# w_out 512 columns wide, eight early pairs, and another first and last chunk in the down stage of a hybrid layer

## The chip, the cores and the metric

The kernel runs on one core of one Trainium2 chip. The metric is the device time of one execution in microseconds (us), as the median of several executions. One further execution is profiled; the rows in this document come from its trace, with times counted from the start of its span. The engines are TensorE (PE, matmuls; PEld is its weight load), VectorE (DVE), ScalarE (ACT), GpSimd (POOL) and SyncE (SP), which here issues nearly all DMAs in the order of its queue.

## What is computed

One post-norm decoder layer on 1024 tokens of width 1024: three token mixers in parallel (a gated linear recurrence, sliding window attention and attention into a memory), their gated sum through `W_out`, a LayerNorm, a squared-ReLU MLP of inner width 4096, and a second LayerNorm. All inputs and outputs are float32. Cut to what the change touches:

```python
merged = (gates[:, :, 0] * (o_a @ w_branch_hg[layer])
          + gates[:, :, 1] * (o_b @ w_branch_swa[layer])
          + gates[:, :, 2] * (o_c @ w_branch_mem[layer]))
mix = merged @ w_out[layer]
h = layer_norm(alpha * h + mix, ln1_g[layer], ln1_b[layer])
ff = jnp.square(jax.nn.relu(h @ w_up[layer])) @ w_down[layer]
h = layer_norm(alpha * h + ff, ln2_g[layer], ln2_b[layer])
```

## The kernel before

**Products.** Every float32 operand is split into a high part, which ScalarE casts (L74), and a low part, the rest, which GpSimd or VectorE subtracts (L75). A product is then three matmuls: high by high, high by low, low by high (`mm`, L59). Two operands of 128x1024 or so therefore cost one cast and one subtraction each before TensorE can use them. SBUF is divided into pools whose names appear in the rows: R holds raw loads (four buffers in rotation), W split weights, X, O, MG, BT and T large operands, G and S small ones; PSUM has three z, three s and two t banks. A tile in a pool's next buffer waits until the tile that held the buffer was last read.

**Mixers, in two halves of 512 tokens** (`hf` = 0, 1): window attention, memory attention, recurrence, then w_out (L627 to L640). There the merged rows stand still in TensorE and the weight passes through 256 columns at a time (`zn`): 384 matmuls per half, four column groups, each added to the residual rows and its statistics taken on VectorE (L636, L640). LayerNorm (L686 to L690) leaves rows with tokens on partitions, and they have to be transposed for the MLP. Each block of 128 rows has a deferred `flip_h1`: for the second half it loads the first half's transposed block from DRAM (L655, "left", an R buffer), transposes its own on TensorE (L661, "right", another R buffer), and forms the sums and differences that the up stage needs on VectorE and GpSimd (L670 to L676 and L75).

**Up stage.** The two token halves and the two halves of a 256 column pair of `W_up` make a 2 by 2 block product, done with seven products of a Strassen type instead of eight: 12 matmuls of 512 columns each, 84 for each of the 16 pairs (L749 to L809). The first two products of a pair use only the plain halves of the tokens. So three pairs (`EARLY`) do their first two products (`first_two`, L726 to L734) ahead of the flips, and keep the first in a PSUM z bank; then all four flips are emitted, then the loop over the pairs. The seven combinations of each pair's result, needed below, go to DRAM as `d_ff[i, j]`.

**Down stage.** Eight chunks of 512 inner columns, again seven products each (`down`, L851; `operands`, L831), 24 matmuls of 512 columns per product, added into eight accumulators `pa[0..7]` of 128x2048. The chunk's w_down rows come raw into two T buffers (`wd_raw`, L822); between products VectorE combines them in place (128x1024, `add`, L710). Per product one left operand is loaded from `d_ff` into R (L833) and split with its low part on GpSimd, and one combination of w_down is split from T. The counter `turn` goes up by two per product, so it is even wherever it is asked, up to the last two products: all left operands before them go to BT buffers, and all weights' low parts to GpSimd. The last chunk orders its products so that the accumulators of the second half's rows are complete first; `finish_rows` normalises them, and the last two products are run row block by row block, each block followed by its LayerNorm (statistics L906 and L943, then L944 to L962, with GpSimd doing a power at L945 and the last addition at L960).

A scheduler orders each engine's queue from dependences; the code above is the order of emission, not of execution.

## Time and profile before

| | us |
|---|---|
| median of 3 runs | 2197.18 |
| fastest, slowest | 2196.35, 2200.23 |
| profiled execution | 2198.1 |
| its span in the trace | 2196.3 |
| TensorE busy in the span | 2089.0 (95%) |
| VectorE, GpSimd, ScalarE busy | 1113.3, 915.3, 844.1 |

The profiled execution has 1.8 us outside its span. Busy shares are means over stages with different limits: TensorE's 95% is nearly 100% in most stretches and much lower in a few, GpSimd's 42% is 94% in the down stage. A stage's own stretch has to be read to see what limits it. The stages of interest begin at about 1430 us (w_out of the second half), 1476 (early pairs), 1493 (flips), 1535 (loop over pairs), 1821 (down stage) and 2106 (last chunk).

### The profile page before, as it was taken

The page shows a single profiled execution, that of the slowest core. Times are in us where ns is not written, and L with a number is a line of the kernel's source. Part 1 is how long each engine was busy: PE and PEld are TensorE (multiplying, and loading weights), DVE is VectorE, ACT ScalarE, POOL GpSimd, SP SyncE. Part 2 cuts the span into 40 slices and gives each one's busy share as a digit, 9 for nine tenths or more (in the row PEclk, how much of TensorE's full clock was granted, in tenths as well). Part 3 has the DMA queues.
Part 4 walks back from the last instruction along what each step waited for, and adds up shares of the span by engine and source line. Part 5 has one row for each costly group of instructions (what it writes and reads, how often), then busy time and mean ns, then how long its engine had stood idle before and what let it go on. Part 6 is the DMA issues. An engine that isn't in the chain of part 4 may idle for free.

```text
span 2196.3 us, 27345 instructions
## 1 busy us (share of the span) xinstructions
PE 2089.0 (95%) x10602; PEld 1741.6 (79%) x10602; DVE 1113.3 (51%) x2032; ACT 844.1 (38%) x1484; POOL 915.3 (42%) x431
## 2 busy tenths in 40 slices
PE   8999999999999999999999999995999997999982
PEld 8767888898988976688889898893888885888872
DVE  5466242244543466634125444237555553676679
ACT  5344243233333254424224333324555554433321
POOL 2212223422235431122332223554344336999984
PEclk9999999999999999999999999996999998999996
DMA  8311223222224441122332223424444448444412
GB/s 286 122 58 58 92 88 99 96 79 85 79 95 126 162 145 48 58 89 87 99 100 80 83 81 94 155 76 148 159 154 158 154 145 301 146 155 152 136 58 77
DMA packets 100114, 256.06 MB, mean 117 GB/s; under 512 B 8544, under 2 KB 22032, under 8 KB 99984
## 3 DMA queue, kind: packets, MB, share of 16 engines
q1 hardware_dynamic: 99088, 251.16, 35.4%
q10 hardware_dynamic: 896, 3.16, 0.4%
q8 instruction: 83, 1.36, 0.3%
q14 instruction: 47, 0.39, 0.1%
HBM read 212.33 MB, written 41.96 MB: 116 GB/s over the span
## 4 chain that ended last, share of the span: by engine, by line
PE 79%; POOL 9%; DVE 5%; issue 5%; ACT 1%; DMA 1%; SPq 0%; DVEq 0%; POOLq 0%; ACTq 0%
PE pz L59 56%; PE ps L59 17%; POOL W L75 5%; PE pt L59 4%; POOL BT L75 2%; PE pt L272 1%; POOL sm L945 1%; DVE X L710 0%; DVE S L264 0%; ACT BT L74 0%; DVE bn L906 0%; POOL X L960 0%; DVE sm L954 0%; DMA T<-in_w_down_dram 0%; PE pt L528 0%
## 5 line engine op out<-in xcount | busy, mean ns | idle before, releaser
L75 POOL TENSOR_TENSOR W<-R,W 128x1024 fp32r<-128x1024 f32 x198 | 478.1, 2415 | 1037.6 <-ACT W L74 1029.9
L59 PE MATMUL pz<-X,W 128*128 128x512 f32 x3360 | 814.9, 396 | 0.0
L59 PEld LDWEIGHTS pz<-X,W 128*128 128x128 f32 x3360 | 624.9, 189 | 140.4 <-issue 11.5
L74 ACT CAST W<-R 128x1024 fp32r<-128x1024 f32 (+1 forms) x299 | 306.0, 1025 | 386.6 <-PE pz L59 158.2
L59 PE MATMUL pz<-O,W 128*128 128x512 f32 x1152 | 266.8, 390 | 0.0
L59 PEld LDWEIGHTS pz<-O,W 128*128 128x128 f32 x1152 | 215.9, 188 | 45.6 <-issue 0.8
L59 PE MATMUL ps<-W,BT 128*128 128x256 f32 (+1 forms) x1016 | 224.0, 340 | 20.1 <-ACT W L74 13.6
L59 PEld LDWEIGHTS ps<-W,BT 128*128 128x128 f32 x1016 | 175.8, 191 | 42.2 <-ACT W L74 14.0
L75 DVE TENSOR_TENSOR W<-R,W 128x1024 fp32r<-128x1024 f32 (+1 forms) x103 | 129.6, 1259 | 116.5 <-ACT W L74 110.4
L75 POOL TENSOR_TENSOR W<-T,W 128x1024 fp32r<-128x1024 f32 x55 | 147.7, 2687 | 21.3 <-ACT W L74 21.3
L75 POOL TENSOR_TENSOR BT<-R,BT 128x1024 fp32r<-128x1024 f32 x55 | 141.4, 2571 | 23.0 <-ACT BT L74 23.0
L59 PE MATMUL pz<-W,BT 128*128 128x512 f32 x492 | 125.9, 391 | 3.0 <-POOL BT L75 2.5
L74 ACT CAST BT<-R 128x1024 fp32r<-128x1024 f32 (+1 forms) x59 | 60.4, 1024 | 168.1 <-issue 134.5
L59 PE MATMUL ps<-W,T 128*128 128x256 f32 x640 | 121.3, 283 | 0.0
L59 PEld LDWEIGHTS pz<-W,BT 128*128 128x128 f32 x492 | 92.9, 189 | 23.3 <-POOL BT L75 2.9
L373 DVE SCALAR_TENSOR_TENSOR G<-G,pz 128x512 f32<-128x512 f32 x32 | 22.0, 687 | 169.9 <-PE pz L59 169.9
L59 PEld LDWEIGHTS ps<-W,T 128*128 128x128 f32 x640 | 97.3, 192 | 1.2
L59 PE MATMUL pz<-W,X 128*128 128x256 f32 x768 | 93.7, 283 | 0.0
L59 PE MATMUL pt<-O,W 128*128 128x512 f32 x384 | 92.6, 390 | 0.8 <-DVE T L710 0.8
L59 PEld LDWEIGHTS pz<-W,X 128*128 128x128 f32 x768 | 92.9, 192 | 0.3
L59 PEld LDWEIGHTS pt<-O,W 128*128 128x128 f32 x384 | 71.9, 188 | 16.6 <-DVE T L710 1.8
L59 PE MATMUL pt<-W,BT 128*128 128x512 f32 x324 | 84.2, 395 | 0.0
(228 smaller groups left out, 2629.0 us busy)
## 6 DMA issues: line engine op xcount, KB each, us to landing
R<-d_ff SPq DMA_DIRECT2D x56, 512.0 KB, 3.6
R<-in_w_gate_dram SPq DMA_DIRECT2D x48, 512.0 KB, 3.6
R<-in_w_b_dram SPq DMA_DIRECT2D x48, 512.0 KB, 3.5
R<-in_w_up_dram SPq DMA_DIRECT2D x35, 512.0 KB, 4.1
T<-in_w_down_dram SPq DMA_DIRECT2D x16, 1024.0 KB, 5.2
d_ff<-T SPq DMA_DIRECT2D x61, 256.0 KB, 2.9
d_ff<-S SPq DMA_DIRECT2D x48, 256.0 KB, 2.9
R<-in_w_sq_dram SPq DMA_DIRECT2D x16, 512.0 KB, 3.6
```

Source lines behind the costliest of these rows:

```text
L59: nc.tensor.matmul(o, lhsT=l, rhs=r, start=start, stop=stop, skip_group_check=more)
L74: (hi_copy or nc.scalar.copy)(hi, src)
L75: (lo_eng or nc.gpsimd).tensor_tensor(out=lo, in0=src, in1=f32(hi), op=ALU.subtract)
L272: nc.tensor.transpose(o[:, c:c + P], pr[:, 2 * t + i, :], ident)
L373: nc.vector.scalar_tensor_tensor(out=t, in0=t, scalar=1.0, in1=o, op0=ALU.add, op1=ALU.mult)
L945: nc.gpsimd.tensor_tensor(out=y, in0=e, in1=mhalf[:, :1], op=ALU.pow)
```

## The change

1. w_out is laid out 512 columns wide: two column groups of four weights, 192 matmuls of 512 columns per half instead of 384 of 256. Two loads of the next stage's tokens (`load_x`) move to the ends of the two groups, and the statistics are taken over 512 columns.
2. `EARLY` goes from 3 to 8. The first product of an early pair no longer stays in PSUM: it is written to DRAM (`d_p1`) and read back in the loop, where VectorE adds it (`plus`) in place of ScalarE's copy. Two flips are emitted ahead of pair 3, two ahead of pair 4.
3. The first chunk of w_down goes into an X buffer. The accumulators are grouped otherwise, their residual rows are loaded after the first product's operands, and GpSimd subtracts one accumulator from another once (128x2048).
4. `turn` goes up by one per product: left operands alternate between BT and MG, the weights' low parts between GpSimd and VectorE.
5. The last chunk is done by plain products, one row block after the other: 8 blocks of 24 matmuls, 192 in place of 168, each followed by its LayerNorm. The combinations of the accumulators move into the seventh chunk, the scale and shift vectors are loaded later, and the last two pairs write one more result (`d_ff[i, 0]`) to DRAM.

```diff
+EARLY = 8
...
-        for cg in range(4):
-            oo = [pt("s"), pt("s")]
-            for c in range(2):
-                w = weight(a["w_o"][2 * cg + c])
-                zn(oo, w, c, mhi[c], mlo[c])
...
+        for f in range(2):
+            oo = [pt("ssst"[n] if f == 0 else "zzzt"[n]) for n in range(4)]
+            cols = slice(f * 512, (f + 1) * 512)
+            for c in range(4):
+                w = weight(a["w_o"][4 * f + c])
+                for n in range(4):
+                    ts = slice(n * P, (n + 1) * P)
+                    for e in range(2):
+                        k = 2 * c + e
+                        rh, rl = w[:, 0, e * 512:(e + 1) * 512], w[:, 1, e * 512:(e + 1) * 512]
+                        lh, ll = mhi[k // 4][:, k % 4, ts], mlo[k // 4][:, k % 4, ts]
+                        mm(oo[n], lh, rh, k == 0, False)
+                        mm(oo[n], lh, rl, False, False)
+                        mm(oo[n], ll, rh, False, k == NK - 1)
+            load_x(nsrc, f + 2, nx, nc.vector)
+            for n in range(4):
+                rv = r[n // 2][:, n % 2, cols]
+                nc.vector.scalar_tensor_tensor(out=rv, in0=rv, scalar=2.0 * ALPHA, in1=oo[n], op0=ALU.mult,
+                                               op1=ALU.add)
+                nc.vector.bn_stats(out=bn[n][:, f, :], in_=rv)
...
+        nc.sync.dma_start(d_p1[i], s1)
...
-        deferred.pop(0)()
+
+    for i in range(EARLY):
+        if i in (3, 4):
+            deferred.pop(0)()
+            deferred.pop(0)()
+        first_two(i)
...
+            p1 = st("G", [P, TH])
+            nc.sync.dma_start(p1, d_p1[i])
...
+        o = pt("z")
         if i >= EARLY:
-            o = pt("z")
...
+        prod(o, w4, 0, 6, i < EARLY)
+        s2 = snap(o) if i >= EARLY else plus(o, p1)
         c = pt("s")
         prod(c, w2, 1, 4)
         prod(o, w3, 0, 7, False)
-        s3 = snap(o)
+        s3 = snap(o) if i >= EARLY else plus(o, p1)
...
+            if i >= NFF - 2:
+                nc.sync.dma_start(d_ff[i, 0], f[:, 2, :])
...
     def wd_raw(c):
-        res = []
+        src = a["w_down"][4 * c:4 * c + 4].rearrange("(j m) p d -> m p j d", m=2)
+        if c == 0:
+            t = st("X", [P, 2, 2, 2, TH])
+            res = [t[:, 0], t[:, 1]]
+        else:
+            res = [st("T", [P, 2, 2, TH]) for _ in range(2)]
         for m in range(2):
-            t = st("T", [P, 2, 2, TH])
-            nc.sync.dma_start(t.rearrange("p j f d -> p j (f d)"),
-                              a["w_down"][4 * c:4 * c + 4].rearrange("(j m) p d -> m p j d", m=2)[m])
-            res.append(t)
+            nc.sync.dma_start(res[m].rearrange("p j f d -> p j (f d)"), src[m])
...
-        t = turn[0]
+        if c == 0 and j == 1:
+            acc_pair("X", 1, 2)
+            rows_h1(2, 0, 0)
+            acc_pair("O", 5, 3)
+            rows_h1(5, 1, 1)
+            rows_h1(3, 0, 1)
+            acc_pair("O", 7, 6)
+            nc.gpsimd.tensor_tensor(out=pa[3], in0=pa[3], in1=pa[5], op=ALU.subtract)
+        if c == 0 and j == 4:
+            acc_pair("X", 4, 0)
+            rows_h1(0, 1, 0)
...
-            o = block(f, w, b)
-            if c == 0 and j in (2, 3, 4):
+            o = psum(turn[0] + b)
+            bs = slice(b * P, (b + 1) * P)
+            for jj in range(2):
+                mm(o, f[:, 0, jj, bs], w[:, 0, jj, :], jj == 0, False)
+                mm(o, f[:, 0, jj, bs], w[:, 1, jj, :], False, False)
+                mm(o, f[:, 1, jj, bs], w[:, 0, jj, :], False, jj == 1)
...
-        turn[0] = t + 1
...
-        down(c, 2, b21)
-        down(c, 5, b11)
+        if c < NC - 2:
+            down(c, 2, b21)
+            down(c, 5, b11)
+            add(b12, b22, b12, ALU.subtract)
+            down(c, 3, b22)
+            down(c, 7, b12)
+            add(b22, b22, b11, ALU.subtract)
+            down(c, 6, b22)
+            add(b21, b21, b22, ALU.subtract)
+            down(c, 4, b21)
+            if c == 1:
+                nc.vector.scalar_tensor_tensor(out=pa[4], in0=pa[0], scalar=ALPHA, in1=pa[4], op0=ALU.mult,
+                                               op1=ALU.add)
+            continue
         add(b12, b22, b12, ALU.subtract)
+        down(c, 7, b12)
         down(c, 3, b22)
-        down(c, 7, b12)
         add(b22, b22, b11, ALU.subtract)
         down(c, 6, b22)
+        add(pa[6], pa[6], pa[1])
+        add(pa[7], pa[7], pa[6])
+        down(c, 2, b21)
         add(b21, b21, b22, ALU.subtract)
+        down(c, 5, b11)
+        add(pa[6], pa[6], pa[5])
+        add(pa[5], pa[5], pa[7])
         down(c, 4, b21)
...
+        add(pa[4], pa[4], pa[7])
+
+    lng, lnb = ln_consts(nc, st, a["ln2_g"], a["ln2_b"])
+    ffs, wds = [], []
+    for j in range(2):
+        for m in range(2):
+            i = NFF - 2 + j
+            raw = st("R", [P, 2, TH])
+            nc.sync.dma_start(raw[:, 0], d_ff[i, (1, 2)[m]])
+            nc.sync.dma_start(raw[:, 1], d_ff[i, (0, 4)[m]])
+            f = st("MG" if m else "BT", [P, 2, S], F32R)
+            split(f[:, 0], f[:, 1], raw.rearrange("p h t -> p (h t)"), nc.gpsimd)
+            ffs.append(f)
+            wds.append(weight(a["w_down"][2 * i + m], nc.vector if m else nc.gpsimd))
+    add(pa[3], pa[3], pa[6])
     add(pa[2], pa[2], pa[1])
...
+    for b in (4, 5, 6, 7, 0, 1, 2, 3):
+        bs = slice(b * P, (b + 1) * P)
...
+        parts = []
+        for ch in range(2):
+            cs = slice(ch * TH, (ch + 1) * TH)
+            o = psum(turn[0])
+            turn[0] += 1
+            for e in range(4):
+                mm(o, ffs[e][:, 0, bs], wds[e][:, 0, cs], e == 0, False)
+                mm(o, ffs[e][:, 0, bs], wds[e][:, 1, cs], False, False)
+                mm(o, ffs[e][:, 1, bs], wds[e][:, 0, cs], False, e == 3)
+            v = pa[((2, 3), (4, 5))[b // 4][ch]][:, b % 4, :]
+            add(v, v, o)
+            nc.vector.bn_stats(out=bn[:, ch, :], in_=v)
+            parts.append((v, cs))
+        layer_norm(nc, small, parts, bn[:, 0:2, :], lng, lnb, LN_EPS, mhalf,
+                   lambda cs, v, b=b: nc.sync.dma_start(outv[b][:, cs], v), b != 3)
```

The scheduler's queues show where this puts the work. First SyncE around the flips. Before (L655 loads a flip's left block, L718 a raw w_up weight, L742 and L754 store and reload results), from the second flip's load on:

```order
L655 DMA R_1470_11891<-d_h1t_82 128x8x128
L742 DMA d_ff_81<-G_1465_11857 128x512
L655 DMA R_1474_11920<-d_h1t_82 128x8x128
L754 DMA T_1482_11978<-d_ff_81 128x512
L754 DMA T_1492_12059<-d_ff_81 128x512
L655 DMA R_1478_11949<-d_h1t_82 128x8x128
L718 DMA R_1483_11979<-in_w_up_dram 128x1024
L718 DMA R_1484_11982<-in_w_up_dram 128x1024
L718 DMA R_1493_12060<-in_w_up_dram 128x1024
```

After, the same place (L663 is the flip's load, L731 the weight, L744 and L750 store the early pairs' two results):

```order
L663 DMA R_1470_11495<-d_h1t_83 128x8x128
L750 DMA d_ff_81<-G_1465_11461 128x512
L731 DMA R_1474_11524<-in_w_up_dram 128x1024
L766 DMA T_1512_11777<-d_ff_81 128x512
L663 DMA R_1480_11563<-d_h1t_83 128x8x128
L663 DMA R_1484_11592<-d_h1t_83 128x8x128
L744 DMA d_p1_82<-G_1477_11542 128x512
L731 DMA R_1488_11621<-in_w_up_dram 128x1024
L731 DMA R_1494_11660<-in_w_up_dram 128x1024
L750 DMA d_ff_81<-G_1479_11558 128x512
L766 DMA T_1524_11861<-d_ff_81 128x512
L731 DMA R_1500_11699<-in_w_up_dram 128x1024
```

One weight load (R_1474, pair 3) now stands ahead of the loads of the third and fourth flip, and those of pairs 4 to 6 behind them.

Second, GpSimd where the up stage ends, the low halves of left operands (BT, MG) and weights (W). Before, from the last up weight (W_1714) on:

```order
L75 TENSOR_TENSOR W_1714_13969<-R_1709_13952,W_1714_13969 128x1024
L75 TENSOR_TENSOR BT_1735_14134<-R_1734_14132,BT_1735_14134 128x1024
L75 TENSOR_TENSOR BT_1742_14175<-R_1741_14173,BT_1742_14175 128x1024
L75 TENSOR_TENSOR W_1736_14137<-T_1732_14128,W_1736_14137 128x1024
L75 TENSOR_TENSOR W_1743_14178<-T_1733_14130,W_1743_14178 128x1024
```

After, from the last up weight (W_1740) on:

```order
L76 TENSOR_TENSOR W_1740_13622<-R_1735_13605,W_1740_13622 128x1024
L76 TENSOR_TENSOR MG_1764_13824<-R_1763_13822,MG_1764_13824 128x1024
L76 TENSOR_TENSOR MG_1778_13905<-R_1777_13903,MG_1778_13905 128x1024
L76 TENSOR_TENSOR BT_1754_13776<-R_1753_13774,BT_1754_13776 128x1024
L76 TENSOR_TENSOR BT_1771_13864<-R_1770_13862,BT_1771_13864 128x1024
L76 TENSOR_TENSOR W_1755_13779<-X_1752_13771,W_1755_13779 128x1024
L76 TENSOR_TENSOR W_1772_13867<-X_1752_13771,W_1772_13867 128x1024
L76 TENSOR_TENSOR W_1786_13948<-X_1752_13771,W_1786_13948 128x1024
L868 TENSOR_TENSOR O_1757_13784<-O_1757_13784 128x2048
```

Two MG operands are made first, then two BT operands, and the first three weights are taken from X instead of T; the accumulators' subtraction (L868) follows them.

Third, TensorE in the last chunk. Before, where the last two products go by row blocks (BT and MG are their left operands; a row "x6" is six matmuls):

```order
L59 MATMUL ps_2153_16461<-W_2149_16450,BT_2148_16447 128x512 x6
L59 MATMUL pt_2154_16469<-W_2152_16458,MG_2151_16455 128x512
L59 MATMUL pz_2160_16498<-W_2149_16450,BT_2148_16447 128x512 x6
L59 MATMUL ps_2161_16506<-W_2152_16458,MG_2151_16455 128x512
L59 MATMUL pt_2167_16535<-W_2149_16450,BT_2148_16447 128x512 x6
L59 MATMUL pz_2168_16543<-W_2152_16458,MG_2151_16455 128x512
L59 MATMUL pz_2175_16580<-W_2152_16458,MG_2151_16455 128x512
```

After, from the last product of the seventh chunk (ps_2111) on:

```order
L60 MATMUL ps_2111_15792<-W_2107_15765,BT_2106_15762 128x512 x6
L60 MATMUL ps_2131_15852<-W_2117_15813,BT_2115_15808 128x512 x3
L60 MATMUL ps_2131_15852<-W_2121_15824,MG_2119_15819 128x512 x3
L60 MATMUL ps_2131_15852<-W_2125_15835,BT_2123_15830 128x512 x2
L60 MATMUL pt_2132_15867<-W_2117_15813,BT_2115_15808 128x512 x2
L60 MATMUL ps_2131_15852<-W_2125_15835,BT_2123_15830 128x512
L60 MATMUL ps_2131_15852<-W_2129_15846,MG_2127_15841 128x512
L60 MATMUL pt_2132_15867<-W_2117_15813,BT_2115_15808 128x512
L60 MATMUL pt_2132_15867<-W_2121_15824,MG_2119_15819 128x512 x3
L60 MATMUL pt_2132_15867<-W_2125_15835,BT_2123_15830 128x512 x3
```

Each row block's result now gathers 12 matmuls per 512 columns from four left operands and four weights; the first block starts ahead of the third pair of operands, and TensorE alternates between two results until that pair is there.

## Rows read from the trace of the kernel before

**Rows 1.** The page's busy times: us, share of span, instructions.

```profile
PE 2089.0 (95%) x10602; PEld 1741.6 (79%) x10602; DVE 1113.3 (51%) x2032; ACT 844.1 (38%) x1484; POOL 915.3 (42%) x431
```

**Rows 2.** The chain that ended last: share of the span by engine.

```profile
PE 79%; POOL 9%; DVE 5%; issue 5%; ACT 1%; DMA 1%; SPq 0%; DVEq 0%; POOLq 0%; ACTq 0%
```

**Rows 3.** Table by stretch: us, busy us of each engine (instructions), granted clock, DMA.

```profile
1430.00:1476.20 46.20, 46.20 (x386) 46.16 (x385) 15.51 (x28) 9.01 (x9) 20.76 (x10) 1.00 0.26 81
...
1492.57:1541.03 48.46, 21.15 (x81) 15.61 (x80) 35.15 (x43) 25.34 (x42) 19.81 (x11) 0.65 0.45 146
...
1549.40:1563.23 13.83, 13.83 (x61) 11.19 (x60) 6.38 (x11) 7.32 (x11) 4.82 (x2) 1.00 0.66 210
...
1821.20:1854.69 33.49, 18.18 (x69) 14.02 (x69) 13.66 (x12) 12.95 (x17) 17.54 (x7) 0.75 0.83 306
...
1900.00:2000.00 100.00, 100.00 (x443) 82.84 (x442) 66.65 (x84) 37.55 (x38) 94.28 (x38) 1.00 0.46 150
...
2105.95:2196.30 90.35, 45.64 (x169) 35.19 (x167) 76.93 (x115) 19.23 (x24) 57.65 (x34) 0.75 0.18 64
```

**Rows 4.** Timeline of TensorE, up to down: start, us, [idle before <-releaser].

```profile
1811.88 2.88 PE L59 MATMUL pz<-BT,W 128*128 128x512 f32 x12
...
1818.27 3.04 PE L59 MATMUL pt<-O,W 128*128 128x512 f32 x12 [0.78 <-DVE T L710]
...
1834.92 0.79 PE L59 MATMUL ps<-W,BT 128*128 128x512 f32 x1 [13.62 <-ACT W L74]
```

**Rows 5.** Timeline of TensorE around the flips.

```profile
1492.57 1.03 PE L661 MATMUL pt<-cst,T 128*128 128x128 f32 x8
...
1525.12 1.22 PE L59 MATMUL ps<-T,W 128*128 128x512 f32 x2 [18.09 <-ACT W L74]
```

**Rows 6.** Timeline of SyncE's queue, first weights of the main loop.

```profile
1516.25 22.11 SPq L718 DMA_DIRECT2D R<-in_w_up_dram  x7
```

**Rows 7.** Timeline of VectorE, last reads of two flips' left blocks.

```profile
1503.63 0.68 DVE L75 TENSOR_TENSOR T<-R,T 128x512 fp32r<-128x512 f32 x1
...
1517.43 0.69 DVE L75 TENSOR_TENSOR T<-R,T 128x512 fp32r<-128x512 f32 x1
```

**Rows 8.** The page's groups (busy us, mean ns) and DMA issues (KB, us).

```profile
L75 POOL TENSOR_TENSOR W<-R,W 128x1024 fp32r<-128x1024 f32 x198 | 478.1, 2415 | 1037.6 <-ACT W L74 1029.9
...
L74 ACT CAST W<-R 128x1024 fp32r<-128x1024 f32 (+1 forms) x299 | 306.0, 1025 | 386.6 <-PE pz L59 158.2
...
R<-in_w_up_dram SPq DMA_DIRECT2D x35, 512.0 KB, 4.1
```

**Rows 9.** Timeline of GpSimd and SyncE, up to down.

```profile
1815.71 4.76 POOL L75 TENSOR_TENSOR BT<-R,BT 128x1024 fp32r<-128x1024 f32 x2 [8.27 <-ACT BT L74]
...
1826.54 2.16 SPq L826 DMA_DIRECT2D T<-in_w_down_dram  x2
```

**Rows 10.** Groups from 1900 to 2105: count, busy us, mean ns, idle before.

```profile
L710 DVE TENSOR_TENSOR T<-T,T 128x1024 f32<-128x1024 f32 x13 | 25.5, 1962 | 12.8 <-POOL W L75 12.8
...
L710 DVE TENSOR_TENSOR X<-X,pz 128x512 f32<-128x512 f32 x32 | 21.8, 682 | 10.1 <-PE pz L59 10.1
...
L75 POOL TENSOR_TENSOR W<-T,W 128x1024 fp32r<-128x1024 f32 x38 | 101.8, 2678 | 4.6 <-ACT W L74 4.6
```

**Rows 11.** Groups of VectorE in the last chunk, 2105.95 to the end.

```profile
L710 DVE TENSOR_TENSOR O<-O,O 128x2048 f32<-128x2048 f32 x2 | 6.6, 3310 | 0.0
...
L75 DVE TENSOR_TENSOR W<-T,W 128x1024 fp32r<-128x1024 f32 x1 | 1.2, 1167 | 0.0
```

**Rows 12.** Timeline of TensorE in the last chunk, its longest wait.

```profile
2166.06 2.50 PE L59 MATMUL pt<-W,MG 128*128 128x512 f32 x5 [14.23 <-DVE sm L955]
```

**Rows 13.** Timeline of VectorE, aggregates of the last three row blocks.

```profile
2175.30 0.20 DVE L943 BATCH_NORM_AGGREGATE sm<-bn 128x2 f32<-128x12 f32 x1
...
2181.93 0.20 DVE L943 BATCH_NORM_AGGREGATE sm<-bn 128x2 f32<-128x12 f32 x1
...
2187.67 0.21 DVE L943 BATCH_NORM_AGGREGATE sm<-bn 128x2 f32<-128x12 f32 x1
```

88 lines of the change are left out of this document (15 added, 73 removed).

## Prediction

> **What bounds the kernel now.** I read the page first, then one table by stage, then the timelines around each hole it shows. TensorE is busy 95% of the span [rows 1] and carries 79% of the chain of waits [rows 2], so time can be won in two ways only: fewer or denser matmuls, or shorter holes in its stream. The table by stage [rows 3] shows where the holes are. In a full stretch, 61 matmuls of 512 columns take 13.83 us, 226.7 ns each, and that is the price I use. The stretch 1900 to 2000 has no hole. The stretch around the flips (1492.57 to 1541.03) and the last chunk (2105.95 to the end) have large ones, with the mean granted clock at 0.65 and 0.75. A third hole lies where the up stage passes into the down stage: TensorE stands 13.62 us ahead of its first down product [rows 4]. The diff touches all three, and w_out.
>
> **w_out, 512 wide.** Before, 386 matmuls of 256 columns fill 46.20 us [rows 3], 119.7 ns each. Per half 384 × 0.1197 = 46.0 us becomes 192 × 0.2267 = 43.5 us; two halves give −4.9 us. Same operands, same weight bytes; nothing on that path waits in the stretch, so it counts in full.
>
> The Trainium skill ("TensorE: Matmul & The Clock Gate", section "Back-to-back issue gap") puts the warm gap at N/2.4 + 2.5 ns, 109.2 and 215.8 ns; by it the two halves would win 768 × 0.1092 − 384 × 0.2158 = 1.0 us only. The rows here show a fixed part nearer 13 ns per matmul, so halving their number is worth more; its other figure there, 131 ns for N = 512 in a sustained stream, no stretch of this trace comes near.
>
> **The up gap.** Before, from 1492.57 (call it F, when the third early pair is done and the transposes of the flips begin) to 1541.03 there are 48 matmuls, 10.9 us of work in 48.46 us: 37.6 us lost. TensorE waits for the first weight of the main loop, 18.09 us [rows 5], which SyncE could issue only at 1516.25 [rows 6], because its R buffer belongs to a flip whose DVE work ends late. The change puts five more early pairs, 5 × 24 × 0.2267 = 27.2 us of matmuls, into this hole. But their weights go through the same R buffers behind the same flips: pair 3 takes flip 0's left buffer, last read by the DVE operation at 1503.63 (F+11.8 at its end), pairs 4 and 5 those of flip 2, last read by the one at 1517.43 (F+25.5) [rows 7], and by my estimate 2 us later now, since flip 2's own buffer waits for flip 1's. A weight then needs 4.1 us to land, 1.0 us of cast and 2.4 us on GpSimd [rows 8]. So pair 3 starts near F+19 and pair 4 near F+35.6; four pairs at 21.8 us, the first at half clock (the mean granted clock of this hole is 0.65, so I add 2.7 us), end near F+60, and by then the main loop's weights are ready. Lost: 60.1 − 27.2 = 32.9 us. I take 37.6 − 32.9, so −5 us. Bounds: −27 if the whole 27.2 us drops into the hole, +3 if GpSimd serves the new weights late (one 2.4 us operation).
>
> In the main loop an early pair runs 60 matmuls, 13.60 us, and takes 13.83 [rows 3]: five more cost about 0.2 us each, +1 us. The reload of the first product (256 KB) and two DVE adds of 0.68 us in place of ScalarE copies lie under TensorE: DVE is at 6.4 of 13.83 us there.
>
> **Up to down.** TensorE's last up product ends at 1821.2 (U). The first w_down load goes out only at 1826.54 [rows 9], since its T buffers are held by the last pairs; the first product then starts at 1834.92 and runs in pieces: from U to 1854.69 TensorE does 69 matmuls, 15.64 us of work in 33.49 [rows 3], 17.9 us lost. The change loads this chunk into an X buffer, which is free after the last pair's second product, two groups of 2.72 us ahead of the BT group at 1811.88 [rows 4], so near U−15. Load and cast are then hidden. What remains is GpSimd's queue: two MG operands, two BT operands, whose buffer TensorE reads until 1814.76 [rows 4], and only then the first weight's low half. Two BT operands end at 1820.47 now [rows 9]; 2.4 us for the weight behind them give U+1.7. I count 2 us of stall left, −16 us. Bounds −18 (none left) and −10 (X lands late and three GpSimd operations of 2.6 us stand on the path). The GpSimd add of 128x2048 in this chunk is behind the third weight; I cost it at nothing, because MG operands were made ahead, and at 3 us if that cover is gone.
>
> **Steady down stage.** 49 products stay 24 matmuls, 5.44 us. GpSimd goes from two operations of about 2.6 us per product (95% busy) to one and a half, 3.9 us; DVE gets every second weight's low half. DVE per chunk: 28 × 0.682 = 19.1, four T adds at 1.96 as measured beside a busy GpSimd [rows 10], 3.5 weights between 1.17 [rows 11] and the same 1.96: 31 to 34 us of 38.1. So no change, 0; the upper end is rival three.
>
> **Last chunk.** Before, 90.35 us: 168 matmuls (38.1 us), stalls of which the longest is 14.23 us [rows 12], and rows finished at DVE's pace, 5.74 us from one aggregate to the next, then 8.6 us from the last aggregate to the end [rows 13]. After, let D be TensorE's end of chunk 6. Eight rows of 24 matmuls are 43.5 us, 5.4 more than before. The third BT operand can't start before D and its low half comes about 2.4 us late: TensorE ends at D+45.9. DVE still has four PSUM adds (2.7 us), two 128x2048 adds at 3.3 us [rows 11] and a weight's low half left at D, together some 12.5 us; its first aggregate is near D+14.5, seven periods of 5.7 later D+54.4, end D+63. That is 90.35 − 63 = −27 us. Bounds: D+56 if TensorE sets the pace (45.9 + about 10 for one row), D+67 at 6.3 us a row: −34 to −23.
>
> **Sum.** −4.9 − 5 + 1 − 16 + 0 − 27 = −52 us. The profiled execution took 2198.1 us (span 2196.3 and 1.8 around it), 0.9 above the median of the three runs, 2197.18. So 2145 us beside the median.
>
> **Rivals.**
> One: the early pairs fill the whole up gap, −27 instead of −5: 2123 us. For it: weights wait in W buffers ahead, and the flips might go faster with GpSimd free. Against it: SyncE's order puts the loads of pairs 4 to 7 behind the loads of all four flips, and only four R buffers turn there. Chance 0.12.
>
> Two: the win is smaller at both ends of the down stage. If X lands late the boundary gives −10, not −16; if rows run at 6.6 us (the spacing before the one shown, 2175.30 to 2181.93) the tail ends 6 to 7 us later, and the DVE backlog of chunk 6 (four adds of 3.3 us on top of 34 of 38.1) stalls TensorE by some 6 us: +18, 2163 us. Chance 0.15. For it: one of the two spacings shown is 6.63 us, where GpSimd's adds stood beside DVE's work.
>
> Three, on the other side: DVE becomes the bound of the down stage. Each DVE operation with two SBUF inputs would wait out a whole GpSimd operation of 2.6 us. Per product that is 4 × 0.682 + (7.5/7) × (1.17 + 2.6) = 6.77 us against 5.44; 49 products give +65 us, 2210 us, slower. It decides from a mean wait of 1.36 us per operation (2.73 + 1.07 × (1.17 + w) = 5.44). Against it: T adds took 1.96 us in a stretch where GpSimd was 94% busy, a wait of 0.8 us, and GpSimd will be 70% busy. Chance 0.05.
>
> The Trainium skill ("SBUF — State Buffer", section "SBUF: two separate sides") says that the port pair shared by DVE and GpSimd is an exclusive lock for a whole instruction, also when the DVE operation has two SBUF inputs; that is rival three's mechanism. The trace agrees on the kind (1.17 us alone, 1.96 beside GpSimd), not on the price of a full instruction each time.
>
> **How the numbers follow.** The forecast holds 0.68: its own range, from the bounds that can fall together (up gap −12 to +3, boundary −18 to −10, tail −34 to −23), is about 2130 to 2162. To leave out no more than 2 in 10 the range goes to rival one on the low side and past rival two on the high: 2122 to 2166. 0.2% is 4.4 us, about what runs of this kernel tell from no change (they spread over 3.9 us). Slower than that is rival three, 0.05; within it, a steady down stage some 1 us slower per product, 0.02; faster 0.93.
>
> **What would show it.** w_out: 192 matmuls per half at 227 ns. The flips: two TensorE holes, one ahead of the fourth early pair (15 us or more) and one ahead of the fifth, instead of one of 18. The boundary: a wait of some 2 us on GpSimd ahead of the first down product, and the clock not at 0.50. Steady stage: 5.44 us a product, GpSimd near 70%, DVE near 85%. Tail: DVE rows 5.6 to 5.8 us apart and TensorE ended some 17 us ahead of the end. I am wrong if the up gap vanishes, if products in chunks 1 to 6 are spaced by more than 5.5 us, or if TensorE's last matmul lies within 10 us of the end.

## The result, and the profile after

The changed kernel takes 2172.02 us (median of 4 runs, 2170.84 to 2174.51) against 2196.89 for the kernel before on the same chip: a ratio of 0.9885 with a 95% interval of 0.9868 to 0.9902. It is 25 us faster; 52 were forecast, and the time lies above the forecast's range (2122 to 2166).

Let F be the first transposes of the flips, U the end of the last up product, D the end of the seventh chunk (chunk 6 in the code) on TensorE. The profiled span falls from 2196.3 to 2171.3 us, as follows:

| stretch | before | after | difference | forecast |
|---|---|---|---|---|
| start to F (w_out, both halves) | 1492.57 | 1489.20 | -3.4 | -4.9 |
| F to U (flips, up stage) | 328.6 | 328.8 | +0.2 | -4 |
| U to D (seven chunks) | 284.8 | 281.3 | -3.5 | -16 |
| D to the end (last chunk) | 90.35 | 72.0 | -18.35 | -27 |

The 27 us that are missing lie in the last two rows (12.5 and 8.7 us), in F to U (4.2) and in w_out (1.5).

The page's busy times and the chain that ended last [rows 1, 2] are now these; GpSimd has less on the chain and TensorE more:

```profile
PE 2096.4 (97%) x10242; PEld 1725.8 (79%) x10242; DVE 1141.3 (53%) x2041; ACT 827.8 (38%) x1462; POOL 844.8 (39%) x401
...
PE 84%; DVE 5%; POOL 4%; issue 3%; DMA 2%; ACT 2%; SPq 0%; POOLq 0%; DVEq 0%; ACTq 0%
```

The table by stretch of the kernel after (columns as in [rows 3]) has, in this order, w_out of the second half, the gap from the flips to the loop over the pairs, the first 33 us of that loop, the first 38 us of the down stage, its steady part, and the last chunk:

```profile
1426.65:1472.87 46.22, 46.22 (x205) 38.27 (x204) 17.19 (x21) 10.18 (x11) 21.68 (x11) 1.00 0.30 92
1489.20:1547.57 58.37, 39.19 (x153) 30.25 (x152) 38.51 (x41) 33.57 (x54) 30.37 (x15) 0.77 0.59 192
1547.57:1581.00 33.43, 30.11 (x123) 23.60 (x122) 16.15 (x24) 12.45 (x18) 8.19 (x4) 0.95 0.49 172
1817.98:1855.60 37.62, 31.18 (x121) 24.09 (x120) 26.19 (x26) 15.35 (x21) 21.00 (x8) 0.91 0.79 282
1900.00:2000.00 100.00, 100.00 (x436) 81.68 (x436) 88.77 (x98) 36.01 (x36) 72.21 (x27) 1.00 0.46 146
2099.30:2171.30 72.00, 47.98 (x193) 37.73 (x191) 61.37 (x100) 11.69 (x17) 38.51 (x25) 0.86 0.16 61
```

**The up gap.** TensorE around the flips and at the loop's start (the loop begins at 1547.57 with the MG operand):

```profile
1504.88 1.22 PE L60 MATMUL pz<-X,W 128*128 128x512 f32 x2 [5.83 <-ACT W L75]
...
1520.67 1.22 PE L60 MATMUL pz<-X,W 128*128 128x512 f32 x2 [4.26 <-ACT W L75]
...
1547.57 2.96 PE L60 MATMUL pz<-MG,W 128*128 128x512 f32 x12
...
1555.17 4.17 PE L60 MATMUL pz<-BT,W 128*128 128x512 f32 x12 [1.91 <-DVE G L718]
```

The one wait of 18.09 us [rows 5] has become two pieces ahead of the fourth and the fifth early pair, and the early pairs end at F+58.4, as forecast (F+60). But the loop's first pairs now wait too (1.91 us at 1555.17, 1.41 at 1572.27). VectorE and SyncE show on what:

```profile
1545.93 0.33 SPq L731 DMA_DIRECT2D R<-in_w_up_dram  x1
...
1550.29 1.60 DVE L718 TENSOR_TENSOR R<-R,R 128x512 f32<-128x512 f32 x1 [7.09 <-DMA R<-in_w_up_dram]
...
1554.34 0.68 DVE L718 TENSOR_TENSOR G<-pz,G 128x512 f32<-128x512 f32 x1
```

A raw weight lands late, VectorE stands at its subtraction for 7.09 us, and `plus` (1554.34), which TensorE waits for, stands behind that in VectorE's queue. SyncE sent this weight at 1545.93, just when GpSimd was done with the low half of an early pair's weight (1543.51 to 1545.91) and that weight's R buffer came free.

**Up to down.** TensorE, SyncE and GpSimd at the start of the down stage:

```profile
1817.96 0.39 PE L60 MATMUL ps<-W,BT 128*128 128x512 f32 x1
1820.06 1.42 PE L60 MATMUL ps<-W,BT 128*128 128x512 f32 x5 [1.71 <-POOL W L76]
...
1844.74 2.93 PE L60 MATMUL ps<-W,MG 128*128 128x512 f32 x6 [4.28 <-DVE O L880]
```

```profile
1838.79 0.48 SPq L846 DMA_DIRECT2D T<-in_w_down_dram  x1
...
1838.84 4.53 POOL L868 TENSOR_TENSOR O<-O 128x2048 f32<-128x2048 f32 x1 [8.87 <-DMA O<-d_h]
...
1848.56 0.36 SPq L836 DMA_DIRECT2D X<-d_h  x1
1848.97 0.73 SPq L846 DMA_DIRECT2D T<-in_w_down_dram  x1
```

The wait of 13.62 us [rows 4] is down to 1.71, nearly the 2 forecast. Then GpSimd stands for 8.87 us until residual rows have landed, subtracts, VectorE's next evictions (which empty PSUM banks) stand behind that, and TensorE stands for 4.28 us and then runs twelve matmuls at the lower of its two clock levels (granted clock 0.50 from 1844.74 to 1850.03), 5.3 us instead of 2.8. SyncE stands for 9.3 us at the next residual rows (1848.56), whose X buffer the first chunk uses until GpSimd's last split from it ends at 1848.54, with the raw operands of the second chunk behind it. From U to the 15th product it is 88.1 us against 94.4 before, so of the 11.9 us won at the first product 6.3 are left; the five later chunks then take 38.6 to 38.7 us each instead of 38.08, which costs 2.8.

**The last chunk.** TensorE, GpSimd and VectorE around D = 2099.3:

```profile
2101.84 0.50 PE L60 MATMUL ps<-W,BT 128*128 128x512 f32 x1 [0.68 <-POOL W L76]
...
2110.55 0.80 PE L60 MATMUL ps<-W,BT 128*128 128x512 f32 x1 [7.75 <-POOL BT L76]
```

```profile
2092.66 2.40 POOL L76 TENSOR_TENSOR BT<-R,BT 128x1024 fp32r<-128x1024 f32 x1
2097.39 4.39 POOL L76 TENSOR_TENSOR W<-R,W 128x1024 fp32r<-128x1024 f32 x1 [2.34 <-ACT W L75]
2101.75 4.39 POOL L76 TENSOR_TENSOR MG<-R,MG 128x1024 fp32r<-128x1024 f32 x1
2106.10 4.40 POOL L76 TENSOR_TENSOR BT<-R,BT 128x1024 fp32r<-128x1024 f32 x1
```

```profile
2097.26 2.28 DVE L718 TENSOR_TENSOR X<-X 128x2048 f32<-128x2048 f32 x1
2099.47 4.47 DVE L718 TENSOR_TENSOR O<-O,O 128x2048 f32<-128x2048 f32 x1
2103.86 0.67 DVE L718 TENSOR_TENSOR X<-X,ps 128x512 f32<-128x512 f32 x1
2104.46 3.83 DVE L718 TENSOR_TENSOR O<-O,O 128x2048 f32<-128x2048 f32 x1
...
2111.51 2.28 DVE L718 TENSOR_TENSOR X<-X,O 128x2048 f32<-128x2048 f32 x1
2113.71 2.28 DVE L718 TENSOR_TENSOR O<-O,O 128x2048 f32<-128x2048 f32 x1
2117.96 0.69 DVE L718 TENSOR_TENSOR X<-X,ps 128x512 f32<-128x512 f32 x1 [1.97 <-PE ps L60]
...
2120.94 0.20 DVE L977 BATCH_NORM_AGGREGATE sm<-bn 128x2 f32<-128x12 f32 x1
...
2162.81 0.21 DVE L977 BATCH_NORM_AGGREGATE sm<-bn 128x2 f32<-128x12 f32 x1
```

Read the last two fences side by side. A GpSimd operation that takes 2.40 us alone takes 4.4 beside VectorE's 128x2048 additions, and such an addition takes 4.47 or 3.83 us instead of 2.28: the starts and ends fit two engines that run in turn, each standing through the other's operation, while the addition with an operand in PSUM (2103.86) keeps its 0.67. GpSimd's last low half is ready at 2110.5, TensorE waits 7.75 us for it, and the first aggregate starts at D+21.6 (D+14.5 was forecast). Four large additions stand behind D on VectorE (12.9 us together); when they are done, at 2115.99, it waits another 1.97 us for TensorE's first result. So both queues were late at that point.

### The profile page after: what moved, and what is told of

Same layout as the page of the kernel before. It is cut to its first block, busy times and chain, and to the rows that moved or that the text cites. A ratio compares the mean times of both kernels' runs of the same rounds, so it can differ in the third digit from the quotient of the medians.

```text
span 2171.3 us, 26697 instructions
## 1 busy us (share of the span) xinstructions
PE 2096.4 (97%) x10242; PEld 1725.8 (79%) x10242; DVE 1141.3 (53%) x2041; ACT 827.8 (38%) x1462; POOL 844.8 (39%) x401
## 3 DMA queue, kind: packets, MB, share of 16 engines
q1 hardware_dynamic: 102400, 258.24, 36.7%
## 4 chain that ended last, share of the span: by engine, by line
PE 84%; DVE 5%; POOL 4%; issue 3%; DMA 2%; ACT 2%; SPq 0%; POOLq 0%; DVEq 0%; ACTq 0%
PE pz L60 59%; PE ps L60 17%; PE pt L60 7%; POOL W L76 1%; DMA R<-in_w_up_dram 1%; PE pt L274 1%; POOL sm L979 1%; DVE T L718 1%; ACT W L75 1%; POOL BT L76 0%; DVE R L718 0%; POOL O L994 0%; POOL MG L76 0%; DVE S L266 0%; DMA R<-d_ff 0%
## 5 line engine op out<-in xcount | busy, mean ns | idle before, releaser
L60 PE MATMUL ps<-W,BT 128*128 128x512 f32 x360 | 98.9, 392 | 10.1 <-POOL BT L76 7.8
L60 PE MATMUL pz<-W,BT 128*128 128x512 f32 x354 | 97.4, 393 | 0.2 <-DVE X L880 0.2
L76 POOL TENSOR_TENSOR BT<-R,BT 128x1024 fp32r<-128x1024 f32 x27 | 70.0, 2595 | 52.9 <-ACT BT L75 52.9
L60 PEld LDWEIGHTS ps<-W,BT 128*128 128x128 f32 x360 | 67.6, 188 | 25.8 <-POOL BT L76 8.2
L76 POOL TENSOR_TENSOR MG<-R,MG 128x1024 fp32r<-128x1024 f32 (+1 forms) x30 | 78.9, 2632 | 16.5 <-ACT MG L75 16.5
L377 POOL TENSOR_TENSOR MG<-MG,G 128x512 f32<-128x512 f32 x32 | 42.3, 1321 | 99.7 <-DVE G L375 99.7
L60 PEld LDWEIGHTS pz<-W,BT 128*128 128x128 f32 x354 | 67.0, 190 | 15.4 <-DVE X L880 0.7
L60 PE MATMUL ps<-W,MG 128*128 128x512 f32 x252 | 68.2, 402 | 4.3 <-DVE O L880 4.3
L60 PE MATMUL ps<-W,T 128*128 128x256 f32 (+1 forms) x432 | 67.5, 294 | 0.0
L60 PE MATMUL pz<-W,MG 128*128 128x512 f32 x252 | 66.6, 396 | 0.0
```

Source lines behind the costliest of these rows:

```text
L60: nc.tensor.matmul(o, lhsT=l, rhs=r, start=start, stop=stop, skip_group_check=more)
L76: (lo_eng or nc.gpsimd).tensor_tensor(out=lo, in0=src, in1=f32(hi), op=ALU.subtract)
L377: nc.gpsimd.tensor_tensor(out=mg, in0=mg, in1=th, op=ALU.add)
```

## Experiments

Differences are against the changed kernel unless said otherwise, and for a stretch they come from the profiled executions. A ratio is to the kernel before, measured beside each run (0.9885 for the changed kernel). Executions of one kernel lie 2 to 8 us apart, so a single edit worth 1 to 3 us is read from its stretch, not from its time. Stretches scatter too: in the runs below that leave its code alone, F to U takes 327.3 to 329.9 us, the first 14 down products 86.9 to 89.8 and D to the end 70.1 to 72.1.

**w_out alone** (the kernel before with part 1 only).

> The kernel before with one part of the change alone: the w_out products 512 columns wide. By the forecast's term less the 1.1 us that TensorE now stands longer at the first half's end: 3.4 to 4.9 us faster, 2192 to 2193.5 us. Rival (the two half-width products cost hardly more than one full one, because TensorE's stream has no gap between them): under 1.5 us, 2195.5 to 2197 us.

2194.22 us against 2198.21, ratio 0.9981 (0.9972 to 0.9991): 4.0 us, as expected, with an interval of 2 to 6.

**The up gap: three early pairs again.** `EARLY = 3`, the first product in PSUM, all flips behind the early pairs.

> The changed kernel with its second part undone: three early pairs as before, all four flips after them, the first product kept in PSUM. My theory (the up gap was not gained: five more early pairs fill a hole of 37.6 us, but the loop's first pairs then wait for weights that come through the same four R buffers): within 3 us of the changed kernel, 2169 to 2175 us, and from the first transpose to the last up product within 2 us of before's 328.6 us. Rival (the early pairs gained the forecast 4 to 5 us and the loss lies elsewhere): 2176 us or more.

2173.12 us (ratio 0.9892, 0.9873 to 0.9910), and F to U takes 328.4 us, against 328.8 with eight early pairs and 328.6 before. TensorE's wait is back with 18.10 us, and nothing is lost by it: part 2 of the change is worth nothing that these runs could show. What it wins in the gap the first pairs of the loop give back.

**The flips' own blocks out of the R buffers.**

```diff
-            right = st("R", [P, 8, P])
+            right = st("S", [P, 8, P])
```

> The changed kernel with the flips' own blocks (the right ones) in S buffers, which are free once the scale and shift vectors of the first LayerNorm are read, so that R buffers hold raw weights and left blocks alone. Theory (R buffers hold the weights back): the loads of pairs 3 to 7 and of the loop's first pairs are issued earlier, the two holes ahead of pairs 3 and 4 (5.8 and 4.3 us and the half clock behind them) shrink and the loop starts without a wait for its weights: 6 to 15 us less than the changed kernel, 2157 to 2166. Rival (the flips' VectorE work sets the pace, whatever the buffers): within 2 us of 2172.

2168.79 us (0.9874, 0.9858 to 0.9890); F to U falls to 323.8, 5.0 us less and outside the scatter. So the four R buffers, through which flips and weights pass in turn, are a limit of this stretch. It is less than expected, since one wait of 9.67 us stays and the pairs' `plus` still wait (3.45 and 1.51 us).

**The first chunk without the subtraction on GpSimd, and with a later read of the rows.** First, the residual half of accumulators 3 and 5 is added on VectorE in the fourth chunk:

```diff
-            rows_h1(5, 1, 1)
-            nc.gpsimd.tensor_tensor(out=pa[3], in0=pa[3], in1=pa[5], op=ALU.subtract)
-            if c == 0 and j in (2, 3, 5):
+            if c == 0 and j in (2, 3):
+                rows_h1(0, 1, 1)
+            if c == 3:
+                nc.vector.scalar_tensor_tensor(out=pa[5], in0=pa[0], scalar=ALPHA, in1=pa[5], ...)
+                nc.vector.scalar_tensor_tensor(out=pa[3], in0=pa[0], scalar=-ALPHA, in1=pa[3], ...)
```

> The changed kernel without GpSimd's 128x2048 subtraction in the first down chunk: the residual rows that it needs are loaded after the second chunk and added to one accumulator and subtracted from another by VectorE in the fourth chunk (two 128x2048 operations). Theory (the first chunk's 4.28 us wait of TensorE and the half clock behind it, 2.6 us, come from this subtraction, which waits for its rows until 1838.8): 5 to 7 us less, 2165 to 2167. Rival (the rows' late load alone holds the accumulators): the wait shrinks by at most the 4.5 us of the subtraction itself to under 1 us but comes back in chunk 4 through VectorE, total within 2 us of 2172.

2173.18 us (0.9896, 0.9878 to 0.9915). The wait of 4.28 us is gone, but others of 3.00 and 2.58 us stand further on: nothing is won. Second, the load of residual rows into accumulator 0 is asked for in the second chunk (`if c == 1 and j == 3:` ahead of `rows_h1(0, 1, 0)`):

> The changed kernel with one load moved: the residual rows of the last accumulator pair (1 MB into the X buffer that holds the first w_down chunk) are asked for in the second chunk's fourth product, behind the loads of that chunk's weights and left operands on SyncE's queue, in place of ahead of them. Theory (the first two down chunks lose about 11 us over their 14 products whatever single wait is removed, because two holds stand one behind the other: GpSimd's subtraction in chunk 1, and SyncE's queue, which stands some 10 us on this load because its buffer is read until the first chunk's last weight is split): the subtraction's wait stays, the rest shrinks: up end to the 15th product 88 us now, 85 to 88 then; total 0 to 3 us less than 2172. Rival (the stretch is bound by the DMA engines' bandwidth, their share is 0.9 to 1.05 there): no change, within 1 us.

2170.71 us (0.9875, 0.9861 to 0.9890), a wait of 3.14 us stays, and the first 14 products take 86.1 us. Third, both:

> Both edits to the first down chunks at once: no subtraction on GpSimd there (residual added in the fourth chunk by VectorE) and the last accumulator pair's rows asked for behind the second chunk's loads. Theory of two holds: from the up stage's end to the 15th down product 80 to 83 us in place of 88.1, total 5 to 9 us less than the changed kernel, 2163 to 2167. Rival (bandwidth): 87 us or more, total within 2 us of 2172.

2168.85 us (0.9869, 0.9855 to 0.9884). From the first down product to the fifteenth it is 82.05 us instead of 88.13, in the range expected (the time lies just above its own), and these are TensorE's waits of more than 0.3 us from 1814 to 1875:

```profile
1814.57 3.03 PE L60 MATMUL pt<-O,W 128*128 128x512 f32 x12 [0.78 <-DVE T L718]
...
1819.56 1.43 PE L60 MATMUL ps<-W,BT 128*128 128x512 f32 x5 [1.74 <-POOL W L76]
...
1871.52 1.65 PE L60 MATMUL pt<-W,MG 128*128 128x512 f32 x6 [1.22 <-DVE X L718]
```

Two holes stood behind each other: GpSimd's subtraction, and SyncE at the rows whose buffer is in use. With one of them mended the other still showed: 89.9 and 86.1 us lie in or next to the scatter, 82.05 does not.

**The first w_down chunk back in T** (`res = [st("T", ...) for _ in range(2)]` for every chunk).

> The changed kernel with the first w_down chunk back in the T buffers, all else as changed. Theory one (the buffer's move is what ended the 14 to 18 us wait at the first down product): that wait is back with 10 to 16 us, of which the 4.3 us at the subtraction and part of the slow clock go away, so the time is 7 to 13 us longer than changed, 2179 to 2185. Theory two (the down stage's start is bound by the partial rows that come back from HBM, whichever buffer the weight has): the same 10 us are lost anyway, 0 to 3 us longer, 2172 to 2175.

2172.57 us (0.9882, 0.9865 to 0.9900), the same as changed. More telling than the time: the wait did not come back. SyncE sends the first weight at U-6.9 though it goes to a T buffer.

```profile
1813.22 1.04 SPq L842 DMA_DIRECT2D T<-in_w_down_dram  x1
...
1822.28 0.50 PE L60 MATMUL ps<-W,BT 128*128 128x512 f32 x1 [2.04 <-ACT W L75]
```

Theory one is refuted: the new buffer did not end the wait; the time is theory two's. Whether SyncE's order ended it is tested in the kernel before.

**Before, with the rows' loads behind the first weight.** The four loads of residual rows (L817) are asked for after the first product's operands; all else as before.

> The kernel before, with only the loads of the four residual rows of the down stage asked for behind the first product's operands instead of ahead of the first w_down chunk. Theory one (in the kernel before the first weight waited because SyncE had the rows' loads and the last pair's results ahead of it, not for its T buffer): SyncE sends the first weight near U-8 (U = end of TensorE's last up product) instead of U+5.4, the wait of 13.6 us before the first down product falls to under 4, a part of it comes back at the third product, which needs the rows, and the time is 5 to 12 us under before, 2185 to 2192. Theory two (the T buffers are held by the last pairs, as the forecast has it): the wait stays over 10 us and the time within 2 us of before.

```profile
1812.68 1.63 SPq L824 DMA_DIRECT2D T<-in_w_down_dram  x2
...
1823.17 2.35 PE L59 MATMUL ps<-W,BT 128*128 128x512 f32 x5 [1.92 <-POOL W L75]
...
1845.88 2.93 PE L59 MATMUL pz<-W,BT 128*128 128x512 f32 x6 [6.07 <-DVE X L858]
...
1857.81 1.22 PE L59 MATMUL ps<-W,BT 128*128 128x512 f32 x2 [2.60 <-ACT BT L74]
1860.25 2.08 PE L59 MATMUL ps<-W,BT 128*128 128x512 f32 x4 [1.22 <-POOL BT L75]
```

The weight goes out at U-8.2 into the same T buffers, and the wait of 13.62 us is 1.92. On the mechanism theory one holds; part 3 of the change moved these loads too, and the forecast gave that no price. On the time it misses: 2198.91 us against 2197.68, ratio 1.0006 (0.9996 to 1.0015). The third product waits 6.07 us for rows that now come later, the fifth 2.60 and 1.22 us for operands whose loads stand behind those rows.

**MG left operands.** In the steady part six matmuls take 1.40 us from an MG operand and 1.36 to 1.37 from a BT operand (233.2 and 227.9 ns each):

```profile
1859.81 1.56 PE L60 MATMUL ps<-W,MG 128*128 128x512 f32 x6
1861.21 1.53 PE L60 MATMUL pt<-W,BT 128*128 128x512 f32 x6
1862.58 1.52 PE L60 MATMUL pz<-W,BT 128*128 128x512 f32 x6
```

All in BT (`f = st("BT", ...)`):

> The changed kernel with the left operands of all 49 down products in BT buffers again; the weights' low halves go on alternating between GpSimd and VectorE. Theory (a matmul whose left operand lies in MG takes 233.2 ns against 227.9 from BT in the same stretch, by the place of the operand): all products at 226.7 to 228 ns, 24 x 24 x 5.5 ns = 3 us less, 2169; chunks 3 to 6 at 38.1 to 38.3 us each in place of 38.65. Rival (the slower matmuls come from VectorE's or GpSimd's accesses in those products, since the weight's low half is VectorE's there): the same 233 ns in every second product, no change; a loss if two BT buffers no longer cover a product.

2172.86 us (0.9885, 0.9868 to 0.9901). Chunks 3 to 6 take 38.1 to 38.3 us instead of 38.6 to 38.7, so the theory holds at some 0.5 us a chunk. But with one pair of buffers new waits of 2.58 and 3.09 us eat it up; the seventh chunk alone takes 43.8 us.

**The last operands in T**, so that their casts need not wait for D:

```diff
-            f = st("MG" if m else "BT", [P, 2, S], F32R)
+            f = st("T" if j else "MG" if m else "BT", [P, 2, S], F32R)
```

> The changed kernel with the last chunk's third and fourth left operands in T buffers, which are free there, in place of a BT and an MG buffer that the seventh chunk's last products still read. Theory one (TensorE's wait of 7.75 us in the last chunk is the BT buffer's, and the end follows TensorE): wait under 2 us, 5 to 7 us less, 2165 to 2167. Theory two (VectorE is saturated from the seventh chunk's end on by the 128x2048 additions, which wait for GpSimd and make it wait, and sets the end): the wait shrinks, but the end moves by 0 to 3 us, 2169 to 2172.

2170.92 us (0.9885, 0.9870 to 0.9900). The wait goes from 7.75 to 6.13 us only, and D to the end is 69.7 us, 2.3 less, as theory two has it: the buffer is the smaller part.

**Two large additions to GpSimd**, early in the seventh chunk.

> The changed kernel with two of the six 128x2048 additions of accumulators taken from VectorE's queue around the end of the seventh chunk and done by GpSimd in the middle of that chunk. Theory (VectorE's queue, saturated from 2085 to 2116, sets the first row block's aggregate, 21.6 us after the seventh chunk's end, and by it the end): first aggregate 3 to 6 us earlier against that chunk's end, total 3 to 6 us less, 2166 to 2169. Rival (TensorE's wait of 7.75 us on GpSimd's left operand sets it): that wait shrinks by under 2 us and the end moves by under 2 us; a loss if the two GpSimd additions (4.5 us each) stall products of the seventh chunk.

2179.03 us (0.9920, 0.9903 to 0.9938), 7 us slower. The additions take 4.6 us each on GpSimd, and TensorE waits 7.33 us for VectorE within the seventh chunk, with 5.36 left in the last.

**Two of the large additions left out** (`pa[3] += pa[6]`, `pa[2] += pa[1]`; four of the eight row blocks lack their share).

> The changed kernel without the two 128x2048 additions that gather four of the seven partial sums into two (so four eighths of the last products lack their share; part of the computation is left out). Theory one (VectorE and GpSimd hold each other up in the last 20 us): VectorE has 8.3 us less to do before the last chunk's aggregates, GpSimd makes the right operands in about 2.4 us instead of 4.4, TensorE's wait of 7.75 us before the low half of rows shrinks to under 4, the first aggregate ends 15 to 18 us behind TensorE's last product of chunk 6 instead of 21.6, and the end comes 3 to 7 us earlier: 2165 to 2169 us. Theory two (TensorE waits for a buffer, whatever VectorE does): the wait stays over 6 us and the time stays within 2 us of 2172.

2168.12 us (0.9860, 0.9845 to 0.9875), but by the trace D to the end is only 2.8 us shorter (69.2), and the wait is 6.69 us: the time is theory one's, the wait theory two's. GpSimd's three operations still took 4.52, 4.40 and 3.32 us, because other large additions moved beside them. So all of them were left out, seven in number:

> The changed kernel without all seven 128x2048 additions that put the eight sums together (left out, so the rows are not the layer's result). Theory one (each GpSimd operation of the last chunk waits out one large VectorE addition, 2.4 + 2 us): GpSimd's last three operations take 2.4 us each instead of 4.4, the last BT operand is ready 5 to 6 us earlier, TensorE's wait of 7.75 us falls to 2 to 3, the first aggregate ends 12 to 15 us behind TensorE's last product of chunk 6 instead of 21.6, and the end comes 5 to 8 us earlier: 2164 to 2167. Theory two (the low half is late because its buffer and its cast are, whatever VectorE does): the wait stays over 6 us, the time within 3 us of 2172.

```profile
2096.87 2.41 POOL L76 TENSOR_TENSOR W<-R,W 128x1024 fp32r<-128x1024 f32 x1 [3.14 <-ACT W L75]
2099.24 2.40 POOL L76 TENSOR_TENSOR MG<-R,MG 128x1024 fp32r<-128x1024 f32 x1
2102.37 2.37 POOL L76 TENSOR_TENSOR BT<-R,BT 128x1024 fp32r<-128x1024 f32 x1 [0.73 <-ACT BT L75]
...
2104.80 0.50 PE L60 MATMUL ps<-W,BT 128*128 128x512 f32 x1 [1.26 <-POOL BT L76]
...
2109.80 0.21 DVE L970 BATCH_NORM_AGGREGATE sm<-bn 128x2 f32<-128x12 f32 x1
```

2162.99 us (0.9841, 0.9822 to 0.9860). Now GpSimd takes 2.4 us for each, TensorE waits 1.26 instead of 7.75 us and ends at D+46.3 (D is 2101.0 here), the first aggregate starts at D+8.8 and D to the end is 59.8 us. Theory one holds, beyond its numbers: the wait is made by the two engines standing through each other's operations. The earlier aggregate and end are not this alone, since VectorE also has the work of the additions less.

**The low halves of the last two left operands on VectorE** (`nc.vector if j else nc.gpsimd` in their `split`).

> The changed kernel with the low halves of the last two left operands made by VectorE instead of GpSimd. Theory one (the two engines hold each other up): GpSimd has two operations of 4.4 us less, VectorE three large additions that no longer wait (2.28 instead of 3.8 to 4.5) against two subtractions of 1.2 more; TensorE's wait goes from 7.75 to 4 to 6.5, the end 2 to 4 us earlier, 2168 to 2170. Theory two (VectorE's own queue is the length that counts): the operand stands behind the same additions, wait and end within 1 us, 2171 to 2173.

2171.17 us (0.9881, 0.9862 to 0.9900). TensorE's wait falls to 3.00 us and its last matmul ends 51.7 us behind D instead of 56.4, but the first aggregate is at D+21.3, as changed: the work now stands in VectorE's queue. On the end theory two is right.

**Mends together.** First four (flips in S, last operands in T, residual rows of accumulator 0 in the second chunk, the other residual in the fourth), then the first, third and fourth with the lows on VectorE and the last two large additions asked for behind two row blocks:

> The changed kernel with four mends found so far: flips' right block in the S buffers, the last chunk's operands in T, the second read of partial rows asked for in chunk 2, and the subtraction of chunk 1 moved. Each brought 1 to 6 us by itself. Theory one (they stand at different places of the one chain of TensorE, so they add): 10 to 14 us faster than changed, 2158 to 2162. Theory two (what is gained ahead of a stage is lost at its end, as between the flips and the up loop): 3 to 6 us, 2166 to 2169.

> Flips' right block in S, second read of the rows in chunk 2, the residual added later, the last two left operands' low halves on VectorE, and two of the large additions asked for behind two row blocks. Theory one: as e12 (2164.8) and 1 to 4 us better at the end, 2160 to 2164. Theory two (what is taken from GpSimd comes back on VectorE): 2164 to 2167.

2164.76 us (0.9851, 0.9830 to 0.9871) and 2163.35 us (0.9846, 0.9829 to 0.9864). Both beat the changed kernel: every run of theirs is faster than every run of it. In the second F to U is 325.6 us, U to D 275.7, D to the end 69.5: 3.2, 5.6 and 2.5 us less than changed. Of the 5.0 us that the flips' buffers won alone 3.2 are left. The first fell short of its 2158 to 2162: a wait of 3.00 us stands at 1868 in its second chunk, one of 6.13 us in the last, and the four had not brought 1 to 6 us each, as the expectation says, but between 1 us lost and 3 us won.

## Why the prediction was wrong

**w_out: right.** -4.9 forecast, -4.0 alone. The price behind it, 0.2267 us a matmul, was read as 13.83 / 61, but the window holds 60 matmuls and the end of another. It is right by luck: twelve take 2.72 us (1811.88 [rows 4] to the next group at 1814.60).

**Up gap: a step failed.** The sum said that the early pairs end near F+60, "by then the main loop's weights are ready". The first half came true (F+58.4). The weights were not ready: five more pairs' weights use the same four R buffers, so the loop's come later, and in its first 33.43 us it does 123 matmuls, 27.9 us at 0.2267. The 31.2 us lost ahead of the loop and these 5.5 make 36.7, against 37.6 before; the rest of the loop loses 1 us more, as much as the forecast's +1 for five more reloaded pairs. The kernel with three early pairs shows the same total. So the sum set unlike things against each other: the 37.6 us before are 32.6 ahead of the loop and 5.0 in its first 48 matmuls, the 32.9 us after end with the early pairs. A stretch that feeds through a rotation of buffers ends when the rotation has caught up.

**Boundary: the effect at the first product right, its mechanism and its total wrong.** "Since its T buffers are held by the last pairs" is refuted twice: with T buffers the wait is 2.04 us in the new order, and 1.92 in the kernel before with its rows' loads moved. [rows 9] showed a load at 1826.54 and I took the reason from the buffers; what stood ahead of it in SyncE's queue was the reason. And "I cost it at nothing", said of the GpSimd subtraction, failed with its cover: GpSimd stood 8.87 us for the row. It and SyncE's stand at the next row cost 6.1 us together (82.05 against 88.13), behind each other, where 3 were the upper price. With both mended U to D is 275.7 us; the forecast's -16 on 284.8 is 268.8. Of the 6.9 us between, about 3 are the MG operands (24 of 49 products × 24 matmuls × 5.3 ns = 3.1), which "49 products stay 24 matmuls, 5.44 us" left out. The rest, some 4 us, lies mostly in the first two chunks, 41.6 and 40.4 us there against 38.6 for the third; what holds them beyond their waits of 1.71 and 1.24 us was not taken apart.

**Steady stage: right in kind.** VectorE is at 88.8% and GpSimd at 72.2% of 100 us, TensorE at 100%, and rival three did not come. But a product takes 5.52 us in the mean, 5.59 from MG: the prediction's own sign of being wrong (5.5) is just passed.

**Last chunk: the order of work right, three terms mis-sized.** Of the 9 us missing, 7.1 are in the first aggregate (D+21.6, not D+14.5) and 2.0 in the rows behind it. TensorE was to wait about 2.4 us for the third operand and end at D+45.9; it waited 7.75 + 0.68 us and worked 47.98 instead of 43.5 (granted clock 0.54 in the 6.45 us after the wait, and MG), and ended at D+56.4. With no large additions its last matmul ends at D+46.3, so what that sum lacked was the meeting of the two engines: three of GpSimd's operations at 4.4 instead of 2.4 us (+6). The first aggregate was put at D+14.5 with two large additions of 3.3 us left at D. Four were left, of 4.47, 3.83, 2.28 and 2.28 us: 12.9 in place of 6.6. The terms named for VectorE also add up to 10.5 us, not to 12.5. The period of the rows came out at 5.98 us ((2162.81 - 2120.94) / 7) instead of 5.7.

The prediction quoted the rule of the Trainium skill that speaks to this ("SBUF — State Buffer", section "SBUF: two separate sides": the pair of ports that VectorE and GpSimd share is held for a whole instruction) and set its price aside, because T additions took 1.96 us in the mean. The mean hid two kinds. In the kernel before, from 1900 to 2105, thirteen of the 24 T additions took 1.21 to 1.23 us and eleven, which started while a GpSimd operation was under way, 2.82 to 2.83:

```profile
1905.39 1.22 DVE L710 TENSOR_TENSOR T<-T 128x1024 f32<-128x1024 f32 x1 [2.55 <-POOL W L75]
...
1907.13 2.83 DVE L710 TENSOR_TENSOR T<-T,T 128x1024 f32<-128x1024 f32 x1
```

The 3.31 us of [rows 11] is such a mean too, of 4.34 and 2.28. Where the operations of both engines follow each other without a break, as here, the trace comes near the full price: 2.28 and 2.40 us alone make 4.68, and VectorE's took up to 4.47, GpSimd's 4.39 to 4.40.

Rival two (2163 us, 0.15) was nearest in kind, a smaller win at both ends of the down stage. Its three parts came out otherwise: the boundary gave less than its -10 (-3.5), the tail cost 9 us more where it had 6 to 7, and its stalls of 6 us in the seventh chunk did not come (38.59 us, like the chunks before). The time went beyond it because the up gap gave nothing either.

## What to carry to other kernels

A load that goes out late can be explained by what stands ahead of it in its queue as well as by its buffer: read that queue's rows from the last issue backwards before a price is put on another buffer. When a hole is filled with work that draws on the same buffers as what comes after it, count to the point where the rotation has caught up. Where VectorE and GpSimd both run long operations with SBUF operands, price a meeting at up to the sum of both, not at a mean over the stage, and count every operation that the new order leaves in the queue.

## What was not expected of the hardware

Matmuls of the same shape take 233.2 ns each with the left operand in one buffer (MG) and 227.9 in another (BT), steadily over seven chunks, and 226.7 in the kernel before, where all left operands of these products were in BT. Putting them back shortens a chunk by some 0.5 us. That alone leaves open whether it is the buffer or the alternation between two, but the up stage of the kernel before, which this edit does not touch, shows the same of MG, there as the operand that passes through: twelve matmuls take 2.80 us from MG, 2.72 from BT.

```profile
1806.35 2.95 PE L59 MATMUL pz<-MG,W 128*128 128x512 f32 x12
1809.15 2.90 PE L59 MATMUL ps<-T,W 128*128 128x512 f32 x12
```

So it goes with the buffer; what of the buffer makes it so, no run here shows.
